# The recurrence's mixer: sums of neighbours and low parts of all mixes moved from GpSimd to VectorE

## The chip, the cores and the metric

The kernel runs on one core of a Trainium2 chip. A core has TensorE (PE in the profile; PEld is its weight load), VectorE (DVE), ScalarE (ACT), GpSimd (POOL) and SyncE (SP, which here only issues transfers). Each engine takes its instructions in the order of its own list, and semaphores hold an instruction until what it reads is there. The metric is device time in microseconds (us) for the whole program, less is better.

## The reference

Two trunk layers over 512 latent tokens with a prefix of 256 context tokens, width 1024. Layer 1 has a bidirectional RWKV-7 mixer between two half feed-forwards. What the change touches is the input side of that mixer: every token is mixed with the mean of its two neighbours, by six learned vectors, before the projections.

```python
def token_shift(x):
    xp = jnp.pad(x, ((0, 0), (1, 1), (0, 0)))
    return 0.5 * (xp[:, :-2] + xp[:, 2:]) - x
...
    xx = token_shift(h)
    xr, xw, xk, xv, xa, xg = (h + xx * x_mix[j] for j in range(6))
    r = heads(xr @ w_r)
    k = xk @ w_k
    v = heads(xv @ w_v)
...
        w_pre = (w0[d] + jnp.tanh(xw @ w1[d]) @ w2[d]).astype(jnp.float32)
        a = jax.nn.sigmoid(a0[d] + (xa @ a1[d]) @ a2[d])
...
    g = jax.nn.sigmoid(xg @ g1) @ g2
```

The context tokens go through the same code, apart from the latent ones.

## The kernel before, in words

Activations lie transposed: eight tiles of 128 channels by 768 tokens, of which 256 are context (CTX) and 512 latent (LAT). A product of two fp32 matrices is made of three passes on rounded numbers: each operand is split into a high part (`hi`, a cast to the rounded type) and a low part (`lo`, the number less its high part), and `mmk` issues hi by hi, lo by hi and hi by lo. So whatever PE multiplies needs a cast and a subtraction first. For weights that is `w_split` (L492, a cast on ACT; L497 or L499, the subtraction on DVE), and for the mixes it is `rw_mix`.

The mixer's input is made tile by tile (`kt` is the tile):

- `rw_norm`: `nxr` on DVE (L1662), then `hf`, the normalised and modulated tile, on ACT (L1663).
- `rw_sum` (L1673): the sum of the left and right neighbour, into the tile `xx` (named `sh` in the trace), on POOL; the two edge columns are copied on ACT (L1674, L1675).
- `rw_diff` (L1682): half the sum less `hf`, on DVE.
- `rw_mix(j, kt, groups, eng)`: for each group the product and sum `mixf` on DVE (L1692), the cast `mixhi` on ACT (L1693), and the subtraction `mixlo` on the engine `eng` (L1696; L1695 is the same, issued later). j is the stream: 0 for r, 1 for the decay, 2 for k, 3 for v, 4 for a, 5 for g.

The code is written in the order in which each engine is to work; nothing reorders it. In program order, with the times of the profile:

- From 2126 us (`rw_begin`): `rw_norm` and `rw_sum` of all eight CTX tiles, beside the last products of the feed-forward (`xb`, L814), then differences and mixes of stream 3, and from 2153 the rest of them in `rwkv_gemm`.
- From 2160: the same for the eight LAT tiles, in a hand-written pipeline `pipe`; a round holds `rw_norm` and `rw_sum` of tile t, then `rw_diff` and `rw_mix` of tile t-1. PE multiplies tile by tile behind it, with the weights of four output tiles. The low part goes to DVE for even and to POOL for odd tiles (`alt`).
- From 2217: during the last two output tiles of v (`pair`), `rw_mix(2, kt)` for both groups, two mixes a tile; tiles 0 to 4 have their low parts on POOL, 5 to 7 on DVE. `v_tr` copies transposed parts of v (`vtok`, L1805) in between. Behind the mix of tile 5, ACT copies the products out (`vt`), which makes room for k.
- From 2301: during the last two output tiles of k, `rw_mix(0, kt)` for LAT, one mix a tile, tiles 0 to 4 on POOL.
- From 2325: the products of r, with the low-rank products of streams 1, 4 and 5 strewn in (`l1(k)`, after the steps of `L1_AT`). After `l1(k)` the next weights are split (`w_pre`) and `l1_mix(k + 2)` makes five mixes: two of 256 and three of 512 columns, all low parts on POOL.

POOL also adds the squares of the norm (`nacc`, L637) until 2149. The buffers of the mixes come from one pool of 45 tiles (`slab`); `l1` gives back a tile's mixes when PE has read them.

Of the kernel before, what the change touches and what calls it, by code (L numbers as in the profile page):

```python
# [10 lines left out]
ALU = mybir.AluOpType  # L11
# [13 lines left out]
LAT = (NCTX, NLAT, 0)  # L25
# [405 lines left out]
class K:  # L431
# [1233 lines left out]
    def rw_sum(self, kt, g):  # L1665

        nc = self.nc
        t0, n, cd = g
        h = self.hf[kt]
        if kt not in self.xx:  # L1670
            self.xx[kt] = self.slab([128, NT], F32, "sh")
        t = self.xx[kt]
        nc.gpsimd.tensor_tensor(t[:, t0 + 1:t0 + n - 1], h[:, t0:t0 + n - 2], h[:, t0 + 2:t0 + n], ALU.add)  # L1673
        nc.scalar.copy(t[:, t0:t0 + 1], h[:, t0 + 1:t0 + 2])  # L1674
        nc.scalar.copy(t[:, t0 + n - 1:t0 + n], h[:, t0 + n - 2:t0 + n - 1])  # L1675

# [40 lines left out]
    def rwkv_gemm(self, st):  # L1717
        nc, A, dp = self.nc, self.A, self.dp
# [4 lines left out]
        self.v_d = dp.tile([NT, D], F32, name="v_d")  # L1723
        self.l_d = dp.tile([3, 128, NT], F32, name="l_d")
        groups = (CTX, LAT)
        alt = lambda kt: nc.gpsimd if kt % 2 else nc.vector
        ident = self.cst("ident", 128)
        while self.tq:
            self.tq.pop(0)()
# [68 lines left out]
        def v_tr(m):  # L1798
            t = vt.pop(m)
            for q0, qn in ((0, 2), (2, 4)):  # L1800
                ps = self.psb()
                for q in range(q0, q0 + qn):
                    nc.tensor.transpose(ps[:, (q - q0) * 128:(q - q0 + 1) * 128], t[:, q * 128:(q + 1) * 128], ident)
                o = self.tp.tile([128, qn, 128], F32, tag="t", name="vtok")
                nc.vector.tensor_copy(o, ps[:, 0:qn * 128].rearrange("p (q e) -> p q e", q=qn))  # L1805
                nc.sync.dma_start(out=self.v_d[q0 * 128:(q0 + qn) * 128, m * 128:(m + 1) * 128].rearrange("(q p) e -> p q e", p=128), in_=o)
# [12 lines left out]
        def pair(n, j, nxt, at):  # L1819

            ws = [self.w_next(("rw", n, m), live=m - 6) for m in (6, 7)]
            pss = [[self.psa() for g in groups] for m in (6, 7)]
            for kt in range(8):
                for w, ps in zip(ws, pss):
                    for p, g in zip(ps, groups):
                        step(p, w, j, kt, g)
                self.mx.pop((j, kt))
                if kt < 6:
                    nxt(kt)
                at(kt)  # L1830
            return pss

        nxt = lambda kt: self.rw_mix(2, kt, groups, nc.vector if kt > 4 else nc.gpsimd)
        pss = pair("v", 3, nxt, lambda kt: {1: lambda: v_tr(4), 3: lambda: v_tr(5)}.get(kt, lambda: None)())
        for m, ps in zip((6, 7), pss):
            for p, g in zip(ps, groups):
# [9 lines left out]
        def out_k(m, pss):  # L1846
            t = self.slab([128, NT], F32, "kt")
            for p, (t0, n, cd) in zip(pss, groups):
                nc.scalar.copy(t[:, t0:t0 + n], p[:, 0:n])
            nc.sync.dma_start(out=self.k_d[m], in_=t)  # L1850
            sq = self.slab([128, NT], F32, "ksq")
            nc.scalar.activation(sq, t, AF.Square, scale=self.col("k_k", m))
            return sq

        def k_stat(m, sq):
            if m == 0:
                kst["ps"] = self.psb(), self.psb()
            o = CC.at["win"] + 14 - 2 * m
            for ps, t0, n_ in zip(kst["ps"], (0, 512), (512, 256)):
                self.mm(ps[0:16, 0:n_], self.cs[:, o:o + 16], sq[:, t0:t0 + n_], start=(m == 0), stop=(m == 7))  # L1860

        pend = []
        for m in range(6):
# [7 lines left out]
            while pend:  # L1871
                k_stat(*pend.pop(0))
            pend.append((m, out_k(m, pss)))
        nxt = lambda kt: self.rw_mix(0, kt, (LAT,), nc.vector if kt > 4 else nc.gpsimd, True)
        pss = pair("k", 2, nxt, lambda kt: k_stat(*pend.pop(0)) if kt == 1 else None)
        for m, ps in zip((6, 7), pss):
            pend.append((m, out_k(m, ps)))
# [16 lines left out]
        def l1_mix(kt):  # L1894
            if kt < 8:
                for i, (j, gs) in enumerate(br):
                    self.rw_mix(j, kt, gs, nc.gpsimd, True)
                self.xx[kt] = self.hf[kt] = None

        def l1(kt):  # L1900
# [21 lines left out]
        for m in range(8):  # L1922
            w = self.w_next(("rw", "r", m))
            ps = self.psa()
            for kt in range(8):
                step(ps, w, 0, kt, LAT)
                if m == 0 and kt in (2, 5):
                    k_stat(*pend.pop(0))
                for k in range(8):
                    if L1_AT[k] == 8 * m + kt:  # L1930
                        l1(k)
                        for _ in range(1):
                            (self.w_pre() or int)()
                        l1_mix(k + 2)
                        if k == 7:
                            l1_out()
                if m == 0 and kt == 6:
                    self.preload(AF.Sqrt)
                    for p, n_ in zip(kst["ps"], (512, 256)):
                        rn = self.tp.tile([16, n_], F32, tag="t", name="rn")  # L1940
                        nc.scalar.activation(rn, p[0:16, 0:n_], AF.Sqrt)
                        self.rn.append(rn)
                    kst.clear()
                    p = None
                if m == 0 and kt == 0:
                    l1_mix(0)
                if m == 0 and kt == 6:
                    for _ in range(1):
                        (self.w_pre() or int)()
                    l1_mix(1)  # L1950
# [1125 lines left out]
```

## Time and profile before

| | us |
|---|---|
| median of 3 runs | 3383.92 |
| lowest and highest run | 3383.01, 3398.22 |
| profiled execution | 3399.75 |
| its span | 3398.0 |
| POOL busy in L1673 and L1696 | 15.4 + 75.7 |
| DVE busy in L1692 | 76.0 |
| stretch from the first sum to the last low part | 2127.4 to 2390.0 |

The times below come from the profiled execution. A row of the timeline is the start, the duration, the engine, the line and operation, what it writes and reads with shapes, how many equal ones are merged, and in brackets how long the engine had been idle and what released it. The group rows give count, busy us and mean ns, then the idle time before them by releaser.

### The profile page before, as it was taken

The numbers are of one execution on the slowest core, as the hardware profiler recorded it, in microseconds if no ns is written. First come the engines' busy times: TensorE is split into PE (matmuls) and PEld (weight loads), VectorE is DVE, ScalarE is ACT, GpSimd is POOL, SyncE is SP. The second block draws the span as 40 slices with busy tenths as digits, with TensorE's granted clock in tenths as the row PEclk, the third lists the DMA queues.
The fourth block names the chain that finished last, engine by engine and source line by source line (L and its number), as shares of the span: only waits on it lengthen the run. The fifth ranks groups of instructions, "written<-read, shape, count | busy, mean of one in ns | idle before, by whom it ended". The sixth has DMA issues, their size and how long they took to land. (4 is left out here: it accounts for less than half of the span.)

```text
span 3398.0 us, 53135 instructions
## 1 busy us (share of the span) xinstructions
PE 3129.9 (92%) x21616; PEld 2624.8 (77%) x21616; DVE 2217.3 (65%) x3738; ACT 1140.5 (34%) x2086; POOL 311.6 (9%) x282
## 2 busy tenths in 40 slices
PE   7999999998999999999999999998885587799999
PEld 6888888875578888888899888776554466678887
DVE  5877744788766776555767776636779684653434
ACT  4122113343443111214322323434754245532222
POOL 1000001100010000002000000315100142320000
PEclk9999999998999999999999999999766688999999
DMA  6444411200133444431111112231687987732222
GB/s 239 146 146 154 141 62 57 92 25 1 44 106 122 145 143 146 148 121 50 56 64 67 69 63 69 91 114 60 184 228 203 206 188 172 181 122 96 96 99 81
DMA packets 251381, 390.68 MB, mean 115 GB/s; under 512 B 67328, under 2 KB 136576, under 8 KB 251136
## 3 DMA queue, kind: packets, MB, share of 16 engines
q1 hardware_dynamic: 251136, 387.28, 37.0%
q8 instruction: 170, 2.79, 0.3%
q14 instruction: 75, 0.61, 0.1%
HBM read 323.24 MB, written 63.96 MB: 114 GB/s over the span
## 5 line engine op out<-in xcount | busy, mean ns | idle before, releaser
L528 PE MATMUL psa<-hhi,whi 128*128 128x512 f32 (+2 forms) x2296 | 798.2, 348 | 9.2 <-ACT whi L492 3.9
L528 PE MATMUL psa<-hlo,whi 128*128 128x512 f32 (+2 forms) x2296 | 798.0, 348 | 2.4 <-POOL hlo L680 2.2
L528 PE MATMUL psa<-hhi,wlo 128*128 128x512 f32 (+2 forms) x2296 | 798.0, 348 | 0.0
L499 DVE TENSOR_TENSOR wlo<-wraw,whi 128x1024 fp32r<-128x1024 f32 (+2 forms) x246 | 293.8, 1197 | 298.5 <-ACT whi L492 298.5
L528 PEld LDWEIGHTS psa<-hhi,whi 128*128 128x128 f32 x2296 | 436.8, 190 | 62.0 <-ACT whi L492 3.9
L528 PEld LDWEIGHTS psa<-hlo,whi 128*128 128x128 f32 x2296 | 437.0, 190 | 57.6 <-POOL hlo L680 4.1
L528 PEld LDWEIGHTS psa<-hhi,wlo 128*128 128x128 f32 x2296 | 436.1, 190 | 49.0
L528 PE MATMUL psb<-ghi,whi 128*128 128x256 f32 (+1 forms) x1232 | 428.9, 348 | 16.0 <-DVE xb L814 12.7
L528 PE MATMUL psb<-glo,whi 128*128 128x256 f32 (+1 forms) x1232 | 427.2, 347 | 0.9 <-DVE glo L377 0.2
L528 PE MATMUL psb<-ghi,wlo 128*128 128x256 f32 (+1 forms) x1232 | 426.3, 346 | 0.0
L492 ACT CAST whi<-wraw 128x1024 fp32r<-128x1024 f32 (+3 forms) x293 | 290.7, 1003 | 255.0 <-PE psb L528 118.5
L528 PEld LDWEIGHTS psb<-ghi,whi 128*128 128x128 f32 x1232 | 232.9, 189 | 49.6 <-DVE xb L814 14.1
L528 PEld LDWEIGHTS psb<-glo,whi 128*128 128x128 f32 x1232 | 232.7, 189 | 30.9 <-DVE glo L377 3.3
L528 PEld LDWEIGHTS psb<-ghi,wlo 128*128 128x128 f32 x1232 | 232.9, 189 | 30.0
L637 POOL TENSOR_TENSOR nacc<-nacc,nsq 128x512 f32<-128x512 f32 (+1 forms) x50 | 56.3, 1125 | 1782.6 <-ACT nsq L633 1777.7
L786 ACT CAST ghi<-fs 128x256 fp32r<-128x256 f32 (+1 forms) x118 | 63.1, 535 | 418.9 <-DVE fs L785 418.9
L777 ACT ACTIVATE fs<-psa 128x256 f32<-128x256 f32 (+1 forms) x116 | 59.7, 514 | 418.8 <-PE psa L528 418.8
L814 DVE SCALAR_TENSOR_TENSOR xb<-psb,mod,xb 128x256 f32<-128x256 f32 (+1 forms) x256 | 148.8, 610 | 54.2 <-PE psb L528 54.2
L563 DVE CUSTOM_DVE_ANT_0 adaj<-adat,sc,vec 128x512 bf16<-128x512 f32 x224 | 167.9, 750 | 15.2 <-DMA adat<-ada 9.5
L563 DVE CUSTOM_DVE_ANT_0 adaj<-adat,sc,mod 128x512 bf16<-128x512 f32 x224 | 167.9, 750 | 6.1 <-DMA adat<-ada 0.5
L235 DVE TENSOR_TENSOR wlo<-wraw,whi 128x1024 fp32r<-128x1024 f32 x70 | 85.6, 1223 | 89.1 <-ACT whi L232 89.1
L785 DVE TENSOR_TENSOR fs<-fs,psa 128x512 f32<-128x512 f32 (+1 forms) x113 | 65.1, 576 | 118.7 <-PE psa L528 116.2
(419 smaller groups left out, 5138.4 us busy)
## 6 DMA issues: line engine op xcount, KB each, us to landing
wraw<-w SPq DMA_DIRECT2D x242, 512.0 KB
adat<-ada SPq DMA_DIRECT2D x256, 256.0 KB
la_d<-AR SPq DMA_DIRECT2D x32, 384.0 KB
kb_d<-KT SPq DMA_DIRECT2D x16, 768.0 KB
lg_d<-G SPq DMA_DIRECT2D x32, 384.0 KB
lhs<-la_d SPq DMA_DIRECT2D x48, 256.0 KB
lhs<-lg_d SPq DMA_DIRECT2D x48, 256.0 KB
kb<-kb_d SPq DMA_DIRECT2D x48, 256.0 KB
```

The source lines that it names most:

```text
L235: TT(lo, x, hi, ALU.subtract)
L492: nc.scalar.copy(hi, raw)
L499: nc.vector.tensor_tensor(lo, raw, hi, ALU.subtract)
L528: self.last = self.nc.tensor.matmul(ps, lhsT=lhsT, rhs=rhs, start=start, stop=stop)
L563: nc.vector.tensor_tensor_reduce(out=junk, in0=t, in1=self.sc[cd][hf], scale=1.0, scalar=o if hf else self.col("ada_b", l * 72 + j), op0=A ...
L637: (eng or nc.gpsimd).tensor_tensor(st["acc"], st["acc"], sq, ALU.add)
L777: nc.scalar.activation(s, ps[:, 0:grp[1]], AF.Silu)
L785: nc.vector.tensor_tensor(s, s, ps[:, 0:n], ALU.mult)
L786: nc.scalar.copy(ghi[:, t0:t0 + n], s)
L814: nc.vector.scalar_tensor_tensor(xs, ps[:, 0:n], self.modc(l, gd, m, cd), xs, ALU.mult, ALU.add)
```

## The change

Four places that chose POOL now choose DVE: the sum of neighbours, and the low part in all mixes.

```diff
-        nc.gpsimd.tensor_tensor(t[:, t0 + 1:t0 + n - 1], h[:, t0:t0 + n - 2], h[:, t0 + 2:t0 + n], ALU.add)
+        nc.vector.tensor_tensor(t[:, t0 + 1:t0 + n - 1], h[:, t0:t0 + n - 2], h[:, t0 + 2:t0 + n], ALU.add)
...
-        alt = lambda kt: nc.gpsimd if kt % 2 else nc.vector
+        alt = lambda kt: nc.vector
...
-        nxt = lambda kt: self.rw_mix(2, kt, groups, nc.vector if kt > 4 else nc.gpsimd)
+        nxt = lambda kt: self.rw_mix(2, kt, groups, nc.vector)
...
-        nxt = lambda kt: self.rw_mix(0, kt, (LAT,), nc.vector if kt > 4 else nc.gpsimd, True)
+        nxt = lambda kt: self.rw_mix(0, kt, (LAT,), nc.vector, True)
...
-                    self.rw_mix(j, kt, gs, nc.gpsimd, True)
+                    self.rw_mix(j, kt, gs, nc.vector, True)
```

The lists of PE, ACT and SP stay as they are. POOL's loses 16 sums and 59 low parts, DVE's gains them. Two places on DVE show where they land. First the start of the LAT half of stream 3, rounds 0 to 3 of the pipeline (`nxr` and `sh` of one tile, then `sh`, `mixf`, `mixlo` of the tile before):

```order
 L1662 TENSOR_TENSOR nxr<-xb_7699,psb 128x512
+L1673 TENSOR_TENSOR sh<-hf 128x510
 L1662 TENSOR_TENSOR nxr<-xb_7701,psb 128x512
+L1673 TENSOR_TENSOR sh<-hf 128x510
 L1682 SCALAR_TENSOR_TENSOR sh<-sh,hf 128x512
 L1692 SCALAR_TENSOR_TENSOR mixf<-sh,vec,hf 128x512
 L1696 TENSOR_TENSOR mixlo<-mixf,mixhi 128x512
 L1662 TENSOR_TENSOR nxr<-xb_7703,psb 128x512
+L1673 TENSOR_TENSOR sh<-hf 128x510
 L1682 SCALAR_TENSOR_TENSOR sh<-sh,hf 128x512
 L1692 SCALAR_TENSOR_TENSOR mixf<-sh,vec,hf 128x512
+L1696 TENSOR_TENSOR mixlo<-mixf,mixhi 128x512
```

The sum, which reads the `hf` that ACT makes of the `nxr` just ahead of it, now stands between that `nxr` and the difference of the tile before; the low parts of odd tiles stand behind their product. The CTX sums land in the same way, each behind its own `nxr`.

Second, one tile of the low-rank streams on DVE, after 2325, with the split of weights ahead of it:

```order
 L497 TENSOR_TENSOR wlo<-wraw,whi 128x1024
 L1692 SCALAR_TENSOR_TENSOR mixf<-sh,vec,hf 128x256
-L1692 SCALAR_TENSOR_TENSOR mixf<-sh,vec,hf 128x512
+L1696 TENSOR_TENSOR mixlo<-mixf,mixhi 128x256
+L1692 SCALAR_TENSOR_TENSOR mixf<-sh,vec,hf 128x512
+L1696 TENSOR_TENSOR mixlo<-mixf,mixhi 128x512
 L1692 SCALAR_TENSOR_TENSOR mixf<-sh,vec,hf 128x256
-L1692 SCALAR_TENSOR_TENSOR mixf<-sh,vec,hf 128x512 x2
+L1696 TENSOR_TENSOR mixlo<-mixf,mixhi 128x256
+L1692 SCALAR_TENSOR_TENSOR mixf<-sh,vec,hf 128x512
+L1696 TENSOR_TENSOR mixlo<-mixf,mixhi 128x512
```

Five products that stood in a row now have a low part between each two, which reads the cast that ACT makes of the product just ahead.

## The prediction

> **What bounds the kernel now.** I read the page's first part, then the groups of the stretch in which the changed lines run, then its windows, and last the timeline engine by engine. The page says whose time counts:
>
> ```profile
> PE 3129.9 (92%) x21616; PEld 2624.8 (77%) x21616; DVE 2217.3 (65%) x3738; ACT 1140.5 (34%) x2086; POOL 311.6 (9%) x282
> ```
>
> PE sets the end, so another engine costs time only where PE waits for it. The groups from 2120 to 2410 us hold every instruction that the change touches:
>
> ```profile
> L1692 DVE SCALAR_TENSOR_TENSOR mixf<-sh,vec,hf 128x256 f32<-128x256 f32 (+1 forms) x80 | 76.0, 991 | 2.2 <-POOL mixlo L1696 1.3
> L1696 POOL TENSOR_TENSOR mixlo<-mixf,mixhi 128x512 fp32r<-128x512 f32 (+1 forms) x59 | 75.7, 1302 | 130.9 <-ACT mixhi L1693 124.0 <-issue 5.0
> ...
> L1673 POOL TENSOR_TENSOR sh<-hf 128x254 f32<-128x254 f32 (+1 forms) x16 | 15.4, 965 | 31.3 <-ACT hf L1663 31.3
> ...
> L1696 DVE TENSOR_TENSOR mixlo<-mixf,mixhi 128x512 fp32r<-128x512 f32 (+1 forms) x17 | 10.7, 628 | 18.4 <-ACT mixhi L1693 18.4
> ```
>
> 59 low parts and 16 sums move from POOL to DVE. The last row is the warning: the 17 low parts that DVE makes already cost 10.7 us of work and 18.4 us of standing still, since each waits for ACT's cast of the high part. The windows show where PE has no room (columns: stretch, its length, busy us of PE, PEld, DVE, ACT and POOL, granted clock, DMA share, GB/s):
>
> ```profile
> 2160.00:2180.00 20.00, 17.61 (x96) 13.99 (x95) 16.38 (x19) 10.07 (x26) 10.13 (x8) 1.00 0.00 0
> ...
> 2280.00:2300.00 20.00, 20.00 (x104) 15.05 (x103) 2.46 (x3) 5.68 (x8) 0.00 (x0) 1.00 0.21 77
> ...
> 2340.00:2360.00 20.00, 17.41 (x75) 14.13 (x76) 17.26 (x17) 9.06 (x17) 15.27 (x13) 0.91 0.24 77
> 2360.00:2380.00 20.00, 15.07 (x62) 11.67 (x61) 15.59 (x15) 9.65 (x18) 16.21 (x14) 0.91 0.18 60
> ```
>
> At 2280 PE is full and DVE nearly empty. At 2160 and from 2340 PE has idle time while DVE works over 15 of 20 us: there DVE paces PE, and there its extra work counts.
>
> **The price of one mix on DVE.** Two places show product, cast and low part undisturbed by POOL, 256 and 512 wide (start, duration):
>
> ```profile
> 2155.29 0.48 DVE L1692 SCALAR_TENSOR_TENSOR mixf<-sh,vec,hf 128x256 f32<-128x256 f32 x1
> 2156.25 0.43 DVE L1696 TENSOR_TENSOR mixlo<-mixf,mixhi 128x256 fp32r<-128x256 f32 x1 [0.47 <-ACT mixhi L1693]
> 2156.59 0.42 DVE L1682 SCALAR_TENSOR_TENSOR sh<-sh,hf 128x256 f32<-128x256 f32 x1
> ...
> 2231.99 0.74 DVE L1692 SCALAR_TENSOR_TENSOR mixf<-sh,vec,hf 128x512 f32<-128x512 f32 x1
> 2233.41 0.69 DVE L1696 TENSOR_TENSOR mixlo<-mixf,mixhi 128x512 fp32r<-128x512 f32 x1 [0.69 <-ACT mixhi L1693]
> 2234.02 0.48 DVE L1692 SCALAR_TENSOR_TENSOR mixf<-sh,vec,hf 128x256 f32<-128x256 f32 x1
> ```
>
> From one start to the next free slot that is 1.30 us (256) and 2.03 us (512), a third of it the wait for ACT. DVE takes its instructions in order, so the next product stands behind the waiting low part; before, it ran during the cast. I take these two prices throughout.
>
> **A, sums of the context half (2126 to 2160).** The chain per tile is nxr on DVE, hf on ACT, sum. Today ACT paces it:
>
> ```profile
> 2126.28 1.74 DVE L1662 TENSOR_TENSOR nxr<-xb,psb 128x256 f32<-128x256 f32 x5 [0.86 <-PE psb L528]
> 2126.74 0.60 ACT L1663 ACTIVATE hf<-nxr,mod 128x256 f32<-128x256 f32 x1 [1.51 <-DVE nxr L1662]
> 2132.51 0.60 ACT L1663 ACTIVATE hf<-nxr,mod 128x256 f32<-128x256 f32 x1
> 2134.17 1.05 ACT L492 CAST whi<-wraw 128x1024 fp32r<-128x1024 f32 x1
> 2133.36 0.75 DVE L814 SCALAR_TENSOR_TENSOR xb<-psb,mod,xb 128x512 f32<-128x512 f32 x1 [0.93 <-PE psb L528]
> 2151.81 1.23 DVE L497 TENSOR_TENSOR wlo<-wraw,whi 128x1024 fp32r<-128x1024 f32 x1 [1.63 <-ACT whi L492]
> 2149.57 0.38 PE L528 MATMUL psb<-mixhi,wlo 128*128 128x256 f32 x1 [1.07 <-DVE wlo L497]
> ```
>
> Eight hf in 0.82 us steps. With the sum behind hf on DVE a step is 0.46 (nxr to hf) + 0.63 (hf and hand-over) + 0.34 (a 256-wide low part to the next start, for the unseen 254-wide DVE sum) = 1.43, eight of them 11.4: DVE is free at 2137.7. Then come xb (0.67 to the next start), diff (0.45) and product (0.48), and on ACT 0.4 for the cast of the high part; the cast of weights behind it, at 2134.17 today, starts at 2139.7, **5.5 us later**. From there to 2160 every wait of DVE but one is for ACT work that itself follows DVE, so the lag stays; PE meets it at 2149.57, where it already waits. Bounds: DVE has five idle places from 2133.36 to 2151.81, 5.2 us in all (first and last quoted); were all of them room, 0.3 is left; with hand-overs 0.1 us longer, 6.5.
>
> **B, the latent half of mix 3 (2160 to 2195).** PE gets one tile per DVE round.
>
> ```profile
> 2160.24 1.28 DVE L1662 TENSOR_TENSOR nxr<-xb,psb 128x512 f32<-128x512 f32 x2
> 2160.95 0.82 ACT L1663 ACTIVATE hf<-nxr,mod 128x512 f32<-128x512 f32 x1 [1.09 <-DVE nxr L1662]
> 2167.16 0.69 DVE L1682 SCALAR_TENSOR_TENSOR sh<-sh,hf 128x512 f32<-128x512 f32 x1
> 2167.88 0.75 DVE L1692 SCALAR_TENSOR_TENSOR mixf<-sh,vec,hf 128x512 f32<-128x512 f32 x1
> 2170.81 0.50 PE L528 MATMUL psa<-mixlo,whi 128*128 128x512 f32 x1 [0.97 <-POOL mixlo L1696]
> 2191.20 1.28 POOL L1696 TENSOR_TENSOR mixlo<-mixf,mixhi 128x512 fp32r<-128x512 f32 x1 [4.05 <-ACT mixhi L1693]
> ```
>
> A round becomes: nxr to the end of hf 1.56, sum 0.60, diff 0.72, mix 2.03 (1.43 to the low part's start and 0.61), together 4.92. From 2160.24: first nxr and sum 2.16, seven rounds 34.4, last diff and mix without nxr 2.85: 39.4, so 2199.7 against today's 2192.5: **+7.2**. The unseen 510-wide sum lies between 0.60 and 0.75 a step, so 7.2 to 8.4; the low end, since it is a plain two-input sum like the low part.
>
> **C, mix 2 (2217 to 2242).** Six tiles of 1.30 + 2.03, and 1.9 for four copies of v between them (0.34 and 0.60 each by the steps above), make 21.9 from 2216.91, where DVE gets to the sixth end at 2234.02 now.
>
> ```profile
> 2216.91 3.84 DVE L1692 SCALAR_TENSOR_TENSOR mixf<-sh,vec,hf 128x256 f32<-128x256 f32 x4
> 2233.70 0.50 PE L528 MATMUL psa<-mixhi,whi 128*128 128x512 f32 x1 [0.77 <-ACT vt L1773]
> 2241.86 0.50 PE L528 MATMUL psa<-mixhi,whi 128*128 128x512 f32 x1 [3.04 <-ACT mixhi L1693]
> ```
>
> 2238.8 less 2234.02 is **+4.8**: ACT's copies vt stand behind the sixth cast, and PE waits for them and then for the eighth cast. Without the copies' 1.9 it would be 2.9; with each tile 0.2 us longer, 6.
>
> **D, mix 0 (2301 to 2324).** Six pairs of 2.03 end at 2313.1; nothing needs them sooner, since the seventh cast stands on ACT behind kt, which waits for PE. **0**; DVE's idle time is the cover, 8.55 us, of which about 2.5 are used. Were a pair 1.2 times as long, the cover would be gone and each further 0.1 us a pair would cost 0.6.
>
> ```profile
> 2300.93 7.15 DVE L1692 SCALAR_TENSOR_TENSOR mixf<-sh,vec,hf 128x512 f32<-128x512 f32 x6
> 2315.53 0.37 ACT L1849 COPY kt<-psa 128x256 f32<-128x256 f32 x1 [6.74 <-PE psa L528]
> 2320.05 0.69 DVE L1696 TENSOR_TENSOR mixlo<-mixf,mixhi 128x512 fp32r<-128x512 f32 x1 [8.55 <-ACT mixhi L1693]
> ```
>
> **E, the mixes of the low-rank products (2325 to 2388).** Each of eight tiles takes five mixes, then a weight split, and PE's next low-rank product waits for that split's cast on ACT, which stands behind the casts of the mixes:
>
> ```profile
> 2324.65 4.88 DVE L1692 SCALAR_TENSOR_TENSOR mixf<-sh,vec,hf 128x256 f32<-128x256 f32 x5
> 2356.10 5.96 DVE L1692 SCALAR_TENSOR_TENSOR mixf<-sh,vec,hf 128x256 f32<-128x256 f32 x5
> 2372.47 5.91 DVE L1692 SCALAR_TENSOR_TENSOR mixf<-sh,vec,hf 128x256 f32<-128x256 f32 x5
> 2332.13 1.23 DVE L497 TENSOR_TENSOR wlo<-wraw,whi 128x1024 fp32r<-128x1024 f32 x1 [2.60 <-ACT whi L492]
> 2388.22 0.62 DVE L499 TENSOR_TENSOR wlo<-wraw,whi 128x384 fp32r<-128x384 f32 x1 [1.64 <-ACT whi L492]
> 2363.71 0.39 PE L528 MATMUL psb<-mixhi,whi 128*128 128x256 f32 x1 [1.86 <-ACT whi L492]
> ```
>
> Today: 63.5 us from 2324.65 to the last split at 2388.2; in the middle two tiles take 16.4 (2356.10 to 2372.47), 8.2 each. After: a tile's mixes are 2 x 1.30 + 3 x 2.03 = 8.69, eight make 69.5. Between them stand four splits of 1024 and six of 384 columns, 4 x 1.14 + 6 x 0.50 = 7.6 (1.23 and 0.62 less the 0.1 by which starts overlap ends), and waits for ACT. Laying ACT's casts of weights (1.05, and by columns 0.5) and result copies (an estimate: 0.5) behind each tile's last cast leaves some 4.5. Together 81.6, **+18.1**. Without any such wait +13.6; with all eight of today's, 13.6 us (first and last quoted, 2.60 and 1.64), +27.2. I stay near the low end, because the low part now fills part of that wait.
>
> **Sum.** 5.5 + 7.2 + 4.8 + 0 + 18.1 = **+35.6 us**. PE is full between these places, so nothing is won back there; that products run shorter without POOL is in the prices. The profiled execution took 3399.75 (span 3398.0), so it would give 3435.4; it is the slowest of what is shown, the three runs being 3383.01 to 3398.22. On their median 3383.92 the forecast is 3419.5, say **3420**.
>
> The five products of a tile take 5.96 us beside POOL and by the rows alone 2 x 0.48 + 3 x 0.75 = 3.21. The Trainium skill, "SBUF — State Buffer", section "Who interferes with whom", says that a VectorE instruction with two SBUF inputs contends with a GpSimd instruction that reads SBUF, the later blocking wholly. The trace agrees; by the rule alone the products' 76.0 us would fall by some 25, and the time with them.
>
> **Rivals.** *Not slower, contention decides.* DVE gets back 76.0 less 32 x 0.48 + 48 x 0.75 = 24.6 us. If that, and not the wait for the cast, paced the loops, a tile in E would take 2 x 0.74 + 3 x 1.28 = 5.3 us of steps, 1.0 of splits and half of today's wait, 0.8: 7.1 against 8.2, for eight some -8. B's rounds of 0.60 + 0.60 + 0.72 + 0.67 + 0.61 = 3.2 would end it after 28 us in place of 32.2, -4: 3372. It decides from the point where the cast is hidden behind another product; the 0.47 and 0.69 in the quoted rows speak against it. Chance 0.06.
>
> *PE hides half.* A's idle places absorb its lag, C's copies fall away before PE's need, and only E's low end is left: about +14, 3398. Chance 0.08; against it stand PE's waits in A, B and C.
>
> *The clock falls too.* In E PE is busy 32.5 of 40 us, 6.6 of each 8.2 us; a round of 10.2 leaves gaps of 3.6 a tile, and windows with gaps of about 2 already show 0.91. Half speed for a third of a round each, eight times, would add up to 13: 3433. Chance 0.10. The Trainium skill's "TensorE: Matmul & The Clock Gate", section "HAM oscillation — how this bites in real kernels", bears on it: idle gaps of over about 3.4 us bring the half clock. The 0.91 here after gaps of 2 to 3 us agrees roughly.
>
> **Numbers.** The forecast has 0.76. The unknown costs run from 0.3 + 7.2 + 2.9 + 13.6 = 24 to 6.5 + 8.4 + 6 + 27.2 = 48, so its own range is 3408 to 3432; the runs' spread of 15 and the clock rival widen it to **3403 to 3440**. Within 0.5% (17 us), about what a measurement of this kernel can tell from no change: faster 0.03, same 0.11, slower 0.86.
>
> **What would show it.** No L1673 or L1696 on POOL; 76 low parts on DVE, each behind a wait of about 0.5 to 0.7 for mixhi, some 55 us in all (18.4 and 21 x 0.47 + 38 x 0.69); products near 0.48 and 0.75; B's rounds at 4.9 and E's at 10.2 us; PE's waits in 2325 to 2425 grown by some 18. I am wrong if products stay as long as now, or if DVE's lag shows without PE waiting longer.

## The result, and the profile after

| | before | after |
|---|---|---|
| median (us) | 3383.92 | 3423.31 |
| lowest to highest of 5 runs | 3383.01 to 3398.22 | 3421.84 to 3429.79 |
| profiled execution, span | 3399.75, 3398.0 | 3423.31, 3421.5 |

The ratio is 1.0106, 95% interval [1.0093, 1.0119]: slower by 1.1%, some 36 us (the medians lie 39 us apart). The forecast was 3420.

The first part of the page after (busy us, share of the span, instructions) shows what was moved: 75 instructions from POOL to DVE, and PE as before.

```profile
PE 3136.6 (92%) x21616; PEld 2628.3 (77%) x21616; DVE 2226.0 (65%) x3813; ACT 1139.6 (33%) x2086; POOL 222.6 (7%) x207
```

DVE's busy time grew by only 8.7 us net (2217.3 to 2226.0). The groups of the stretch from 2120 to 2450 us say why it costs more than that:

```profile
L1692 DVE SCALAR_TENSOR_TENSOR mixf<-sh,vec,hf 128x256 f32<-128x256 f32 (+1 forms) x80 | 51.2, 641 | 0.8
L1696 DVE TENSOR_TENSOR mixlo<-mixf,mixhi 128x512 fp32r<-128x512 f32 (+1 forms) x76 | 45.2, 594 | 52.8 <-ACT mixhi L1693 52.8
L1673 DVE TENSOR_TENSOR sh<-hf 128x254 f32<-128x254 f32 (+1 forms) x16 | 8.9, 558 | 12.4 <-ACT hf L1663 12.4
```

The products run without POOL beside them and need 51.2 us in place of 76.0. But DVE now stands still for 52.8 us ahead of low parts (18.4 before) and for 12.4 ahead of sums. It is idle time behind ACT, far more than work, that grew.

To see where it turned into time, I cut both executions at the same instructions. A runs from the first `nxr` to the first 512-wide `nxr`; B from there to the end of the last low part of stream 3; C from the first product of mix 2 to the end of its last cast; D from the first product of mix 0 to the first product of E; E to the start of the last split of 384 columns. Worked out from the timelines, in us:

| | A | B | B to C | C | C to D | D | E | E to the last copy of r |
|---|---|---|---|---|---|---|---|---|
| before | 33.96 | 32.24 | 24.43 | 24.90 | 59.12 | 23.72 | 63.57 | 17.28 |
| after | 40.32 | 39.59 | 24.42 | 29.68 | 57.70 | 23.66 | 82.17 | 15.98 |
| difference | +6.36 | +7.35 | 0 | +4.78 | -1.42 | -0.06 | +18.60 | -1.30 |
| the sum's term | +5.5 | +7.2 | 0 | +4.8 | 0 | 0 | +18.1 | 0 |

Together +34.3. What lies ahead of A and behind the last copy is not touched by the change, yet it differs from execution to execution: it took 2126.3 and 992.5 us before, 2122.3 and 985.7 after, and between 2121.2 and 2129.6, and 977.1 and 992.5, over all profiles of this study. So the totals of single executions say less than the cuts, which agree where nothing was edited: within 0.2 us in E, within 1 us in A and B.

One round of B on DVE's timeline (start, duration, what it waited for) shows the whole change; the last row opens the next round:

```profile
2174.64 0.68 DVE L1662 TENSOR_TENSOR nxr<-xb,psb 128x512 f32<-128x512 f32 x1
2176.20 0.69 DVE L1673 TENSOR_TENSOR sh<-hf 128x510 f32<-128x510 f32 x1 [0.88 <-ACT hf L1663]
2176.81 0.69 DVE L1682 SCALAR_TENSOR_TENSOR sh<-sh,hf 128x512 f32<-128x512 f32 x1
2177.53 0.75 DVE L1692 SCALAR_TENSOR_TENSOR mixf<-sh,vec,hf 128x512 f32<-128x512 f32 x1
2178.97 0.69 DVE L1696 TENSOR_TENSOR mixlo<-mixf,mixhi 128x512 fp32r<-128x512 f32 x1 [0.68 <-ACT mixhi L1693]
2179.58 0.68 DVE L1662 TENSOR_TENSOR nxr<-xb,psb 128x512 f32<-128x512 f32 x1
```

From one `nxr` to the next 4.94 us, of which DVE waits 1.56, twice for an ACT instruction that itself could only start when DVE had finished the row above. The two engines take turns on one tile: while ACT makes `hf` or `mixhi`, DVE has nothing to do.

E, by the windows over exactly its cut (busy us of PE, PEld, DVE, ACT and POOL, then the granted clock), before and after:

```profile
2324.65:2388.22 63.57, 51.90 (x218) 41.04 (x217) 49.95 (x52) 31.12 (x60) 48.74 (x39) 0.92 0.23 74
```

```profile
2337.64:2419.81 82.17, 61.11 (x225) 46.67 (x223) 53.74 (x92) 31.33 (x60) 0.00 (x0) 0.85 0.18 57
```

DVE works 3.8 us more, in a stretch that is 18.6 longer. PE's idle time grew by 9.4 (11.7 to 21.1); its busy time by 9.2, at a granted clock of 0.85 for 0.92. As before, most of its waits in E end with ACT's casts of weights, which queue behind the last mix; the mix now ends later. Two of them:

```profile
2357.84 0.43 PE L528 MATMUL psb<-mixhi,whi 128*128 128x256 f32 x1 [4.40 <-ACT whi L492]
2367.47 0.39 PE L528 MATMUL psb<-mixhi,whi 128*128 128x256 f32 x1 [2.07 <-ACT whi L492]
```

### The profile page after: what moved, and what is told of

It is laid out like the page before. It is cut to its first block, busy times and chain, and to the rows that moved or that the text cites. A ratio compares the mean times of both kernels' runs of the same rounds, so it can differ in the third digit from the quotient of the medians.

```text
span 3421.5 us, 53080 instructions
## 1 busy us (share of the span) xinstructions
PE 3136.6 (92%) x21616; PEld 2628.3 (77%) x21616; DVE 2226.0 (65%) x3813; ACT 1139.6 (33%) x2086; POOL 222.6 (7%) x207
```

## The experiments

**One part at a time.** Four kernels are the kernel before with one part of the change. `only_e`:

```diff
-                    self.rw_mix(j, kt, gs, nc.gpsimd, True)
+                    self.rw_mix(j, kt, gs, nc.vector, True)
```

> The kernel before with only the five mixes of the low-rank streams (stretch E) on VectorE. My theory, that each low part makes VectorE stand still behind ScalarE's cast: the stretch from the first product of E to its last weight split takes 82 us in place of 63.6, products 0.48 and 0.75 us long, and the stretches A (34.0), B (32.2) and C (25.0) stay as they were; about +18 us in all. The rival, that TensorE hides much of it: the stretch grows, but the whole by less than 8 us.

`only_sums` takes the first hunk of the change alone (the sum of L1673 on VectorE):

> The kernel before with only the sums of neighbours on VectorE. My theory: A (first context nxr to first latent nxr) 40 us in place of 34.0, since a step of the eight is 1.42 in place of 0.82; B (first latent nxr to the end of the last low part of mix 3) 37 to 39 in place of 32.2, since the wait for hf stands in every round, while low parts of odd tiles still contend from GpSimd; C and E as before; about +12 us. The rival, that B's loss comes from the low parts: B within 2 us of 32.2.

`only_alt` takes the second (`alt = lambda kt: nc.vector`):

> The kernel before with only the odd low parts of the latent half of mix 3 on VectorE, the sums still on GpSimd. If the sums make B's loss: B 31 to 35 us against 32.2 (a round of 3.4 us without contention, some 0.5 of contention with the sum), A, C and E as before, the whole within 4 us. If the low parts make it: B 37 us or more.

`only_cd` takes the two lines of `nxt` (mix 2 and mix 0):

> The kernel before with only the low parts of mix 2 (C) and mix 0 (D) on VectorE. My theory: C, from its first product to TensorE's start on the last tile of k's first product, 29.7 us in place of 25.0; D, from its first product to the first product of E, unchanged at 23.7, its extra work lying in VectorE's idle time ahead of the seventh low part (6 us left of 8.6); A, B and E as before; about +5 us. The rival, that D's work is not hidden either: D 25 us or more.

Measured, by the same cuts, each one execution beside one of before of 3384.74:

| | A | B | C | D | E | time |
|---|---|---|---|---|---|---|
| before | 33.96 | 32.24 | 24.90 | 23.72 | 63.57 | 3384.74 |
| only_e | 33.98 | 32.29 | 24.90 | 23.72 | 82.33 | 3403.64 |
| only_sums | 40.33 | 37.80 | 24.87 | 23.73 | 63.66 | 3399.57 |
| only_alt | 33.98 | 29.75 | 24.89 | 23.72 | 63.72 | 3389.67 |
| only_cd | 34.93 | 32.50 | 29.70 | 23.66 | 63.60 | 3393.14 |

(The cuts in the first row are those of the profile of before.) The times are of single executions, so the cuts are what can be read. Each cost sits in its own stretch and has the size that the whole change has there, and D costs nothing. TensorE hides next to nothing of E: from its end to the last copy of r it then takes 15.96 us for 17.28, so 1.3 of 18.8 come back. B is the exception, and there I missed: the low parts of odd tiles alone make it 2.5 us *shorter*, below the 31 to 35 that I expected, the sums alone 5.6 longer, and both together 7.35 longer. In `only_alt` a round takes 3.43 us:

```profile
2166.14 0.68 DVE L1662 TENSOR_TENSOR nxr<-xb,psb 128x512 f32<-128x512 f32 x1
2166.74 0.68 DVE L1682 SCALAR_TENSOR_TENSOR sh<-sh,hf 128x512 f32<-128x512 f32 x1
2167.46 0.75 DVE L1692 SCALAR_TENSOR_TENSOR mixf<-sh,vec,hf 128x512 f32<-128x512 f32 x1
2168.89 0.76 DVE L1696 TENSOR_TENSOR mixlo<-mixf,mixhi 128x512 fp32r<-128x512 f32 x1 [0.69 <-ACT mixhi L1693]
2169.57 0.68 DVE L1662 TENSOR_TENSOR nxr<-xb,psb 128x512 f32<-128x512 f32 x1
```

POOL's sum of this round, in the next row, runs from 2167.75 to 2169.10. Half of it falls into DVE's wait for the cast, and little of it is left when the low part starts, so next to nothing is blocked (low part 0.76 for 0.69):

```profile
2167.75 1.35 POOL L1673 TENSOR_TENSOR sh<-hf 128x510 f32<-128x510 f32 x1 [2.08 <-ACT hf L1663]
```

So B's loss comes from the sums, and the low parts there turn from a gain into a cost only once the sums wait on DVE too. `only_alt`'s total, 4.9 us above before's where I had said 4 at most, does not bear on this: from A to the last copy of r it took 278.5 us for 279.2, so the 4.9 lie outside.

**The wait without the work.** `wait_only` leaves the low parts of E on POOL, and lets DVE read one column behind each cast:

```diff
+            if eng is nc.gpsimd and pool and j in (1, 4, 5):
+                p = self.small.tile([128, 1], F32, tag="pre", bufs=2, name="peek")
+                nc.vector.tensor_copy(p, hi[:, t0 + n - 1:t0 + n])
             eng.tensor_tensor(lo[:, c], f, hi[:, c], ALU.subtract)
```

> The kernel before, low parts of E still on GpSimd, with one more VectorE instruction behind each of the five casts of a tile: it copies one column of the high part (128x1) and so waits for the cast. If VectorE's wait for the cast is what costs: at least 2 x 0.47 + 3 x 0.69 = 3.0 us more a tile in E, and more where GpSimd's low part then blocks the next product, so E takes 80 us or more in place of 63.6 though VectorE gains only some 3 us of work. If VectorE's work is what costs: E within 4 us of 63.6.

E took 94.0 us, 30.4 more than before and 11.8 more than with the change. The groups (2315 to 2440 us; busy, mean ns, idle before):

```profile
L1692 DVE SCALAR_TENSOR_TENSOR mixf<-sh,vec,hf 128x512 f32<-128x512 f32 (+1 forms) x41 | 49.4, 1206 | 0.0
...
L1698 DVE COPY peek<-mixhi 128x1 f32<-128x1 f32 x40 | 6.2, 154 | 25.1 <-ACT mixhi L1693 25.1
```

The copies are 6.2 us of work (I had said 3), the waits 25.1, as many as the 40 low parts of the change have in E (25.1). The products come on top: the 40 of E took 40.8 us before and 48.6 here (the row's 41st lies ahead of E); the added time stands where POOL's low part starts as DVE goes on. So this is not the wait quite alone: copies and longer products are some 14 us of the 30.4. The 16 that are left are waits, with not one low part on DVE. So a loss of that size needs no low part's work on DVE; what the work itself costs, the next run shows.

**The work without the wait.** `defer_e` is the changed kernel, with each low part of E issued behind the next product:

```diff
-            eng.tensor_tensor(lo[:, c], f, hi[:, c], ALU.subtract)
+            fn = lambda lo=lo[:, c], f=f, hi=hi[:, c]: eng.tensor_tensor(lo, f, hi, ALU.subtract)
+            if defer:
+                self.mix_flush()
+                self.dl.append(fn)
+            else:
+                fn()
...
+    def mix_flush(self):
+        while self.dl:
+            self.dl.pop(0)()
...
-                    self.rw_mix(j, kt, gs, nc.vector, True)
+                    self.rw_mix(j, kt, gs, nc.vector, True, defer=True)
```

> The changed kernel, with the low parts of E issued one product later, so that the next product runs during the cast; the same instructions on the same engines. If the wait for the cast makes E's loss: five mixes cost VectorE 2 x 0.74 + 3 x 1.28 = 5.3 us of steps a tile instead of 8.7, and E takes 56 to 62 us in place of 82.2, below the 63.6 of before; the whole 20 to 26 us less than the changed kernel. If the added work on VectorE makes it: E stays at 75 us or more.

E took 59.58 us, 4.0 less than before and 22.6 less than the change; the other cuts stayed as in the change. Four mixes of one tile on DVE's timeline show it: the same instructions, and no bracket left.

```profile
2352.39 0.48 DVE L1692 SCALAR_TENSOR_TENSOR mixf<-sh,vec,hf 128x256 f32<-128x256 f32 x1
2352.78 0.69 DVE L1696 TENSOR_TENSOR mixlo<-mixf,mixhi 128x512 fp32r<-128x512 f32 x1
2353.38 0.75 DVE L1692 SCALAR_TENSOR_TENSOR mixf<-sh,vec,hf 128x512 f32<-128x512 f32 x1
2354.05 0.42 DVE L1696 TENSOR_TENSOR mixlo<-mixf,mixhi 128x256 fp32r<-128x256 f32 x1
2354.38 0.48 DVE L1692 SCALAR_TENSOR_TENSOR mixf<-sh,vec,hf 128x256 f32<-128x256 f32 x1
2354.82 0.69 DVE L1696 TENSOR_TENSOR mixlo<-mixf,mixhi 128x512 fp32r<-128x512 f32 x1
2355.43 0.75 DVE L1692 SCALAR_TENSOR_TENSOR mixf<-sh,vec,hf 128x512 f32<-128x512 f32 x1
2356.09 0.42 DVE L1696 TENSOR_TENSOR mixlo<-mixf,mixhi 128x256 fp32r<-128x256 f32 x1
```

The window over its E, to hold against the two above:

```profile
2337.62:2397.20 59.58, 51.27 (x225) 38.47 (x223) 50.08 (x90) 31.37 (x60) 0.00 (x0) 1.00 0.24 79
```

The median of 7 runs is 3401.26 against 3389.46 for before, ratio 1.0044 [1.0028, 1.006]: A, B and C still cost what they cost.

**All waits hidden.** `defer_all` does this for every mix, and issues each sum one step later:

```diff
         for kt in range(8):
             self.rw_norm(st, kt)
-            self.rw_sum(kt, CTX)
+            if kt:
+                self.rw_sum(kt - 1, CTX)
+        self.rw_sum(7, CTX)
...
-            pipe.append([lat[t - d][i] for i, d in ((0, 0), (1, 0), (2, 1), (3, 1)) if 0 <= t - d < 8])
+            pipe.append([lat[t - d][i] for i, d in ((0, 0), (2, 1), (3, 1), (1, 0)) if 0 <= t - d < 8])
...
-        nxt = lambda kt: self.rw_mix(2, kt, groups, nc.vector)
+        nxt = lambda kt: self.rw_mix(2, kt, groups, nc.vector, defer=True)
```

> The changed kernel with every low part of the mixes issued one product later and every sum one nxr later (in the latent half behind the product of the tile before); the same instructions on the same engines, all arithmetic of the mixer off GpSimd. If the waits make the whole loss: A 33 to 35 us (ScalarE paces it again), B 28 to 32, C 20 to 24, E 56 to 62, and the whole 0 to 15 us faster than the kernel before. If VectorE's added work (some 20 us more busy than before) counts: at least 10 us slower than before.

`defer_psum` is the same with the sums back on POOL (the first hunk of the change undone):

> The version with all low parts and sums issued later (defer_all: A 33.7, B 28.9, C 22.0, E 59.6), with only the sums of neighbours back on GpSimd. If GpSimd beside VectorE costs where both read: B 30 us or more, with diffs or products over 1 us long, and the whole a few us slower than defer_all. If the sums' place does not matter once nothing waits behind them: B and A within 1 us of defer_all's, and the whole within 0.3% of it.

| | A | B | B to C | C | E | median, runs | ratio to before |
|---|---|---|---|---|---|---|---|
| defer_all | 33.70 | 28.91 | 26.43 | 22.02 | 59.57 | 3379.03, 10 | 0.9970 [0.9957, 0.9983] |
| defer_psum | 32.15 | 29.58 | 27.21 | 21.99 | 59.61 | 3379.12, 10 | 0.9972 [0.9961, 0.9984] |

Both are faster than the kernel before by 0.3%, some 10 us, and are the fastest versions that I ran. With all arithmetic of the mixer on DVE, `defer_all` leaves 2.2 us of waits ahead of its 76 low parts and 3.3 ahead of its sums, for 52.8 and 12.4 with the change:

```profile
L1696 DVE TENSOR_TENSOR mixlo<-mixf,mixhi 128x512 fp32r<-128x512 f32 (+1 forms) x76 | 44.8, 589 | 2.2 <-ACT mixhi L1693 1.8
...
L1673 DVE TENSOR_TENSOR sh<-hf 128x254 f32<-128x254 f32 (+1 forms) x16 | 8.9, 554 | 3.3 <-ACT hf L1663 3.3
```

All of `defer_all`'s expected ranges were met. In B the gain is smaller than the cut shows, as PE then needs 2.0 us longer behind the last low part: B and what follows take 55.3 for 56.7 before. For `defer_psum` neither expectation held alone. The contention is there, with low parts of 1.53 us beside POOL's sums:

```profile
2168.54 0.76 DVE L1692 SCALAR_TENSOR_TENSOR mixf<-sh,vec,hf 128x512 f32<-128x512 f32 x1
2169.20 1.53 DVE L1696 TENSOR_TENSOR mixlo<-mixf,mixhi 128x512 fp32r<-128x512 f32 x1
```

It costs 1.45 us in B and what follows it (56.8 for 55.3), and A gives 1.55 back, where POOL takes eight sums off DVE. The times are alike. So it does not matter which engine makes the sums, once nothing waits behind them, and taking GpSimd away is not what made the change slow. Its low parts beside VectorE did cost the kernel before something, and less than the waits: in E, where they kept DVE from waiting too, the 40 products took 40.8 us before and 25.6 in `defer_e`, and E is 4.0 us shorter.

## Why the prediction was right

- **The price of a mix** (1.30 and 2.03 us) held to 0.01: in C after, a tile takes 3.34. Everything else in the sum is this price and its place.
- **A**, forecast 5.5, measured 6.36. A step of the eight took 1.42 for 1.43, and ACT's cast of weights behind them came 5.45 later, as forecast. The 0.9 on top is a reciprocal that waits for ACT's root of the next norm, 0.87 us. ACT waits there for PE (1.03 us), and PE was slow: for the norm's sums and what stands between them it took 5.61 us at a granted clock of 0.50, where it had taken 3.58 at 1.00. The sum had no term for this.

```profile
2149.57:2153.15 3.58, 2.98 (x25) 2.89 (x26) 1.95 (x3) 1.57 (x2) 0.00 (x0) 1.00 0.58 172
```

```profile
2150.97:2156.58 5.61, 5.52 (x26) 5.43 (x26) 3.08 (x5) 1.97 (x3) 0.00 (x0) 0.50 0.73 248
```

```profile
2157.05 0.18 DVE L653 RECIPROCAL nr<-nr 128x4 f32<-128x4 f32 x1 [0.87 <-ACT nr L652]
```

  The same wait stands in `only_cd` and `wait_only`, where A was not edited and took 34.93 and 34.88 us, at the same half clock; in the other unedited ones, at 33.96 and 33.98, it does not. Whether the change brought it or chance did stays open.

- **B**, 7.2 against 7.35, a round 4.94 against 4.92. That the sums carry it was said by the working (1.56 to the end of hf); `only_sums` shows it.
- **C**, 4.8 against 4.78. PE waits for ACT's copies of v, as forecast, 5.57 us:

```profile
2248.19 0.79 PE L528 MATMUL psa<-mixhi,whi 128*128 128x512 f32 x1 [5.57 <-ACT vt L1773]
```

- **D**, 0 against -0.06. The cover shrank from 8.55 to 5.91, 2.6 used where I had said 2.5. Its bound was worked out wrong: the 6 us left over six pairs are 1.0 us a pair, so a pair would have to be 1.5 times as long, not 1.2, to use up the cover.

```profile
2333.04 0.69 DVE L1696 TENSOR_TENSOR mixlo<-mixf,mixhi 128x512 fp32r<-128x512 f32 x1 [5.91 <-ACT mixhi L1693]
```

- **E**, 18.1 against 18.60. What E holds beside mixes and splits came to 5.1 us (82.17 less 77.1), where 4.5 was laid out. `only_e` shows that the loss stands alone, `wait_only` and `defer_e` that it is the waits.
- **"PE is full between these places, so nothing is won back there"** was wrong by 2.7 us: 1.42 came back between C and D, 1.30 behind E. In the first place the windows show how. Before, PE ran at a granted clock of 0.57 from 2242 to 2246, with nearly all of k still ahead of it; after, the half clock fell on 2248 to 2252, and PE then had to wait for the last cast in any case (1.18 us, at 2256.33). The single runs agree: 57.8 us where C was edited, 58.9 to 60.1 where it was not. Behind E it is not the clock, which was 1.00 in both: PE was busy there for 17.2 us before (78 matmuls on record) and 15.8 after (69), since in E's longer stretch it had got further with r.

```profile
2242.00:2246.00 4.00, 3.78 (x16) 3.27 (x17) 1.76 (x2) 0.76 (x1) 0.00 (x0) 0.57 0.24 51
```

```profile
2248.00:2252.00 4.00, 3.81 (x9) 3.04 (x10) 2.58 (x5) 2.85 (x7) 0.00 (x0) 0.50 0.35 131
```

- **The rivals.** That contention decides: its 25 us did come back in the products (76.0 to 51.2), and did not decide, since the condition named for it, a cast hidden behind another product, was not met. Where `defer_e` meets it, E gains 4.0 against before; the rival had put 8 on it. That PE hides half: out by `only_e`, `only_sums` and `only_cd` (its +14 also left out B's 7.2 without a reason). That the clock falls too: it fell, 0.85 in E, but had no price there. DVE's waits in E all end with ACT's casts, none with PE, so PE worked slower inside time in which it would have waited. Its gaps were mostly 2.1 to 2.3 us, not 3.6, and even before, the clock fell to 0.66 (2365 to 2370) though no gap in E was over 3.0.
- Of the marks, "PE's waits in 2325 to 2425 grown by some 18" was half right: PE's idle time in E grew by 9.4, and the rest went into its slower clock.
- The total was closer than its terms: A, B and E took 1.5 us more than forecast, the 2.7 won back stood against it, and some of that closeness is luck.

## What to carry to other kernels

Before an instruction is moved to another engine, look at what it waits for and what stands behind it on the new engine: in an in-order list it is not its duration that is paid but the gap up to its input, and everything behind pays with it. Here 75 instructions added 8.7 us to DVE's busy time, net of the products that ran shorter, and 36 us to the kernel's; issued one step later, with nothing else changed, they made it 0.3% faster than before the move. When a slower engine looks like the brake, try first whether it only ran in another's shadow.

## What the runs showed of the hardware that I had not expected

A DVE instruction with two inputs in SBUF that starts while POOL reads is drawn out even when POOL's instruction is a plain sum. The price was a little less than what was left of that sum: 0.84 us where 0.99 was left (the low part of 1.53 for 0.69 in `defer_psum`, with POOL's sum from 2168.83 to 2170.19), and 0.07 where 0.21 was left (0.76 in `only_alt`, where DVE had waited for a cast during most of the rest). How two such streams stand to each other in time, not how much each has to do, sets the price.
